# ScalarE issues the query and gate writes, and the bias table follows the state-space parameters

## The chip, the cores and the metric

The kernel runs on one core of a Trainium2 chip. The metric is the device time of one execution in microseconds (us), the median over several runs. A profiled execution of the same program gives the trace.

## The reference

One decoder block on 512 tokens of width 1024, in float32. A normalized input is projected to four parts: `u` (512 columns) for a state-space branch (S5), `q` (1024) and `k`, `v` (256 each) for an attention branch, and `gates` (2048). The two branches are gated, merged by one output projection and added to `x`; a second part (product-key experts, PEER) follows, which the change does not touch.

```python
bias = rel_bias_table.astype(jnp.float32)[t5_bucket(jnp.maximum(dist, 0))]
bias = bias.transpose(2, 0, 1).reshape(N_KV_HEADS, Q_PER_KV, ATTN_BLOCK, 2 * ATTN_BLOCK)
...
scores = jnp.where(valid, scores + bias, NEG_INF)
...
bu_re = jnp.einsum('blgc,gpc->blgp', uf, bbar_re)
bu_im = jnp.einsum('blgc,gpc->blgp', uf, bbar_im)
...
_, _, h_re, h_im = lax.associative_scan(
    _complex_scan_combine, (a_re, a_im, bu_re, bu_im), axis=1)
```

The bias depends on the distance of query and key alone: 16 heads by 384 distances, spread to 128 queries by 256 keys.

## The kernel before

Each float32 product is made of three products of a high and a low part (`mm3`, L94 to L96): `hi*hi`, `lo*hi`, `hi*lo`. A weight block of 512 KB is loaded by SP's queue into `raw` (L117, three buffers), ACT casts it to `hi` (L124), and DVE or POOL subtracts to `lo` (L125); hi and lo have three buffers too. A scheduler orders the instructions of each engine before the run, from the order in which the code yields them; each engine then takes its list strictly in order.

The front part, in the order of the code (`front`):

1. `proj_kv` and `rows`: keys, values, and the normalization rows `rx`, `rb`.
2. `bias_table` (L656): three small loads on ACT's queue, a product `rb_p` on PE, an addition on DVE into the tile `rb_m` of 16 partitions by 384 (L666), and one write of `rb_m` to `bias_d` in device memory (L668), each row 128 times over, 3072 KB. `bias_d` is read back at L833 as a skewed table, 2048 KB.
3. `weave` of `proj` and `s5_params` by two rates: `proj_q` (queries; ACT makes `qt` and its square `sq`, L549 and L550, DVE sums, L551, SP's queue writes `qt` to `q_d`, L553), `proj_u` (L495, L500), and `G0` blocks of `proj_gates`; with them the parameters of S5, a long run of small DVE and POOL operations and matmuls `wtr`, `kps` (L417, L426, `tt` L432).
4. `s5_mix`: four chunks, each with eight matmuls `eps` into two PSUM buffers (L449), DVE operations on the tiles `m` (L453 to L472), and matmuls into `yps` (L476, L478). Beside it run the gate blocks, by the rate `G1`. `eps` and `yps` share four PSUM buffers, the gate blocks' `gps` have two of their own.
5. scores, attention, gated linear unit, branches, output projection. Gate blocks that are left run beside the first scores.

`proj_gates` has 16 blocks of 24 products. For each, DVE multiplies `gps` by `rb` into `gt` (L567), ACT takes the tanh (L568), and the block is written to `g_d` (L569). `gt` and `qt` share two buffers (tag e1): a buffer is free when its write has landed.

Memory: the pool `tp` holds the tiles of the parameters (`wrep0` among them) and of the bias table; it is closed when step 3 ends, and the pool `smp` of `s5_mix`, with the tiles `m`, is opened on the same side and takes the same memory.

Of the kernel before, what the change touches and what calls it, by code (L numbers as in the profile page):

```python
# [10 lines left out]
F32 = mybir.dt.float32  # L11
# [20 lines left out]
def run_some(gen, credit, add):  # L32

    credit += add
    while credit > 0:
        c = next(gen, None)
        if c is None:
            return 0.0
        credit -= c
    return credit  # L40


def weave(main, total, other, cost):

    credit = 0.0
    for c in main:
        yield c
        credit += c * cost / total
        while credit > 0:
            c2 = next(other, None)  # L50
            if c2 is None:
                credit = -1e9
                break
            credit -= c2
            yield c2
    yield from other


class Builder:
    RATE_A, RATE_S, RATE_V, RATE_G = 2.2, 0.96, 1.36, 6.0  # L60
    PARTS = 4
    ALONE, MORE, FAR = 96, 2, 6
    G0, S5C, G1, RATE_Q = 0, 70.0, 8.0, 3.0
    DEEP = 3
    AHEAD = 3
    NT0, NT1, KEY = 2, 2, 3
# [474 lines left out]
    def proj_q(self, xh, xl, ssq, qd, pool):  # L541
        nc = self.nc
        ep = self.ep
        for g in range(2):
            def ev_q(j, ps, g=g):
                qt = ep.tile([128, 512], F32, tag="e1", name=self.nm("qt"))
                sq = ep.tile([128, 512], F32, tag="e2", name=self.nm("sq"), bufs=1)
                r = self.rx[:, j:j + 1]
                nc.scalar.activation(qt, ps, AF.Copy, scale=r)  # L549
                nc.scalar.activation(sq, ps, AF.Square, scale=r)  # L550
                nc.vector.tensor_reduce(ssq[:, j, 8 * g:8 * g + 8], sq.rearrange("p (h d) -> p h d", d=64),  # L551
                                        axis=AX.X, op=ALU.add)
                nc.sync.dma_start(out=qd[j, :, 512 * g:512 * g + 512], in_=qt)  # L553
            yield from self.proj_tok(xh, xl, 512 + 512 * g, ev_q)
        rms = pool.tile([128, NT * 16], F32, name="rms")
        nc.vector.tensor_scalar(rms, ssq.rearrange("p a b -> p (a b)"), 1.0 / 64, EPS, op0=ALU.mult, op1=ALU.add)
        self.rq = self.rsqrt(pool, rms, NT * 16).rearrange("p (a b) -> p a b", b=16)

    def proj_gates(self, xh, xl, bg, gd):
        nc = self.nc  # L560
        for m in range(16):
            wh, wl = self.unit_cols(self.i["w_in"], 2048 + m * 128, 128)
            ps = self.gpsum[0].tile([128, T], F32, tag=self.gpsum[1], name=self.nm("gps"))
            for k in range(KD):
                self.mm3(ps, wh[:, k, :], wl[:, k, :], xh[:, k, :], xl[:, k, :], k == 0, k == KD - 1)
            g = self.ep.tile([128, T], F32, tag="e1", name=self.nm("gt"))
            nc.vector.tensor_mul(g, ps, self.rb)  # L567
            nc.scalar.activation(g, g, AF.Tanh, bias=bg[:, m:m + 1], scale=0.5)  # L568
            nc.sync.dma_start(out=gd[m], in_=g)  # L569
            yield 5.2  # L570

    def kv_prep(self, kv, kH, kL, vH, vL, gk):
# [83 lines left out]
    def bias_table(self, pool, dp):  # L656
        nc, I = self.nc, self.i
        tab = pool.tile([32, 16], F32, name="rb_t")
        oh = pool.tile([32, 384], F32, name="rb_o")
        mk = pool.tile([16, 384], F32, name="rb_m")  # L660
        nc.scalar.dma_start(out=tab, in_=I["rel_bias"])
        nc.scalar.dma_start(out=oh, in_=I["bucket_onehot"])
        nc.scalar.dma_start(out=mk, in_=I["band_mask"])
        ps = self.ptr.tile([16, 384], F32, tag="tr", name="rb_p")
        nc.tensor.matmul(ps, tab, oh, start=True, stop=True)
        nc.vector.tensor_add(mk, mk, ps)  # L666
        bd = dp.tile([16, 128, 384], F32, name="bias_d")
        nc.scalar.dma_start(out=bd, in_=mk[:, None, :].to_broadcast([16, 128, 384]))  # L668
        return bass.AP(tensor=bd.tensor, offset=bd.offset + 127, ap=[[383, 128], [128 * 384, 16], [1, 256]])
# [90 lines left out]
    def front(self, hd, ah, ys):  # L760

        tc, nc, I, L = self.tc, self.nc, self.i, self.pool
        R = "right"
        dp = self.dp
        qd = dp.tile([NT, 128, D], F32, name="q_d")
        gd = dp.tile([16, 128, T], F32, name="g_d")
# [23 lines left out]
        with ExitStack() as ss:  # L790
            sp = L(ss, "s5p")
            up = sp.tile([128, 16, 128], F32, name="up")
            self.rx = kp.tile([128, NT], F32, name="rx")
            rb = self.rb

            def rows():
                with tc.tile_pool(name="np", bufs=1, side=R) as np_:
                    xts = [np_.tile([128, D], F32, name=f"n_x{j}") for j in range(NT)]
                    for j in range(NT):
                        nc.sync.dma_start(out=xts[j], in_=I["x"][j * 128:j * 128 + 128, :])  # L800
                    self.rms_rows(np_, xts, self.rx)
                    ps = self.ptr.tile([128, T], F32, tag="tr", name="rb_ps")
                    for j in range(NT):
                        rr = np_.tile([128, 128], F32, tag="rr", name=self.nm("rr"), bufs=2)
                        nc.vector.tensor_copy(rr, self.rx[:, j:j + 1].to_broadcast([128, 128]))
                        nc.tensor.matmul(ps[:, j * 128:j * 128 + 128], rr, self.ident, start=True, stop=True)
                    nc.scalar.copy(rb, ps)

            gates, credit = self.proj_gates(xh, xl, bg, gd), 0.0

            def proj():
                yield from kvs
                yield from self.proj_q(xh, xl, ssq, qd, kp)
                yield from self.proj_u(xh, xl, up)
                for c, _ in zip(gates, range(self.G0)):
                    yield c

            kvs = self.proj_kv(xh, xl, kv, kp, lambda i: self.x_part(i, small["g1"], xh, xl))
            for _ in range(self.ROWS):
                next(kvs)  # L820
            rows()
            with tc.tile_pool(name="tp", bufs=1, side=R) as tp:
                bias_src = self.bias_table(tp, dp)
                S = {}
                for _ in weave(proj(), 82.0 + 5.2 * self.G0, self.s5_params(sp, tp, S), self.S5C):
                    pass
            with tc.tile_pool(name="smp", bufs=1, side=R) as smp:
                for _ in self.s5_mix(smp, S, up, yg):
                    credit = run_some(gates, credit, self.G1)
# [637 lines left out]
```

## Time and profile before

| | |
|---|---|
| median of 3 runs | 1714.58 us (1713.29 to 1715.45) |
| profiled execution | 1712.47 us |
| its span in the trace | 1710.7 us |
| PE busy | 1622.0 us, 95% |
| DVE busy | 1425.3 us, 83% |
| ACT busy | 843.0 us, 49% |
| mean granted clock of PE | 0.986 |

The share of busy time is a mean over stages. The table of stretches gives it stage by stage, with PEclk, the granted clock of PE as a share of full speed. The list of waits says what ended an engine's idle time. In the timeline, a row is an instruction with its start and duration; a bracket gives the idle time ahead of it and what ended that. For a DMA, the view gives the time from issue to landing. An engine with a q behind its name (SPq, ACTq) is the queue from which DMAs are issued.

### The profile page before, as it was taken

How to read it: one execution, taken by the hardware profiler on the slowest of the kernel's cores; microseconds unless marked ns; L12 is line 12 of the kernel's file. 1: busy time of each engine (PE TensorE's matmuls, PEld its weight loads, DVE VectorE, ACT ScalarE, POOL GpSimd, SP SyncE). 2: the span in 40 equal slices, each digit the busy share in tenths (PEclk: the TensorE clock that was granted, in tenths of full speed). 3: DMA queues.
4: the chain of work that ended last, by engine and by line, in shares of the span. 5: the costliest groups of instructions: out<-in, count | busy, mean ns of one | idle time of the engine just before them, and what ended most of it. 6: DMA issues, size and time to landing. Idle time of an engine off the chain costs nothing.

```text
span 1710.7 us, 25112 instructions
## 1 busy us (share of the span) xinstructions
PE 1622.0 (95%) x8831; PEld 1426.4 (83%) x8831; DVE 1425.3 (83%) x2931; ACT 843.0 (49%) x1290; POOL 575.2 (34%) x472
## 2 busy tenths in 40 slices
PE   7789999998999899999899999999999999999998
PEld 5568878786899888898899998888888888888876
DVE  7799768897797999999999767777887777777876
ACT  5256565664565356766678633333333333333332
POOL 2563022233531322222222324344434343334440
PEclk9899999999999999999999999999999999999999
DMA  7823452656654658767769998889989999999885
GB/s 231 154 86 99 129 172 76 191 151 185 221 164 149 229 191 286 259 237 287 277 222 345 355 352 285 304 322 333 362 311 333 325 321 347 328 344 320 308 276 180
DMA packets 236303, 429.62 MB, mean 251 GB/s; under 512 B 17376, under 2 KB 153104, under 8 KB 233104
## 3 DMA queue, kind: packets, MB, share of 16 engines
q1 hardware_dynamic: 174464, 240.73, 42.4%
q0 software_dynamic: 36864, 134.23, 21.7%
q10 hardware_dynamic: 24848, 53.06, 9.5%
q8 instruction: 69, 1.13, 0.3%
q14 instruction: 58, 0.48, 0.1%
HBM read 373.69 MB, written 54.26 MB: 250 GB/s over the span
## 4 chain that ended last, share of the span: by engine, by line
PE 58%; DVE 21%; DMA 3%; issue 2%; ACT 2%; POOL 0%; SPq 0%; DVEq 0%; ACTq 0%; POOLq 0%
PE po L1160 11%; PE po L1161 10%; PE po L1163 10%; PE pa L94 6%; PE pa L96 6%; PE pa L95 6%; DVE lo L125 5%; DVE sp_row L1209 3%; DVE t_s L966 1%; DVE g_oh L1110 1%; ACT hi L124 1%; DVE g_o L1107 1%; DVE g_ol L1109 1%; DVE t_ix L968 1%; DVE t_ix L972 1%
## 5 line engine op out<-in xcount | busy, mean ns | idle before, releaser
L124 ACT CAST hi<-t_raw 128x1024 fp32r<-128x1024 f32 x256 | 269.6, 1053 | 471.7 <-PE pa L95 195.7
L125 DVE TENSOR_TENSOR lo<-t_raw,hi 128x1024 fp32r<-128x1024 f32 x256 | 312.9, 1222 | 64.2 <-ACT hi L124 63.7
L94 PE MATMUL pa<-x2h,hi 128*128 128x384 f32 x1024 | 348.3, 340 | 14.7 <-ACT u_g L1136 12.5
L96 PE MATMUL pa<-x2h,lo 128*128 128x384 f32 x1024 | 348.8, 342 | 10.7 <-DVE lo L125 10.7
L95 PE MATMUL pa<-x2l,hi 128*128 128x384 f32 x1024 | 345.5, 337 | 0.0
L1192 POOL DMA_INDIRECT sp_row<-peer_u,sp_ei x128 | 192.5, 1504 | 407.4 <-DVE sp_row L1209 369.6
L1192 POOL DMA_INDIRECT sp_row<-peer_v,sp_ei x128 | 198.2, 1549 | 359.8 <-DVE sp_acc L1211 331.7
L1160 PE MATMUL po<-hi,v_wh 128*128 128x512 f32 x768 | 303.5, 395 | 3.2 <-ACT v_wh L89 3.2
L1161 PE MATMUL po<-lo,v_wh 128*128 128x512 f32 x768 | 302.5, 394 | 0.0
L1163 PE MATMUL po<-hi,v_wl 128*128 128x512 f32 x768 | 223.4, 394 | 0.0
L94 PEld LDWEIGHTS pa<-x2h,hi 128*128 128x128 f32 x1024 | 194.2, 190 | 21.3 <-ACT u_g L1136 15.1
L96 PEld LDWEIGHTS pa<-x2h,lo 128*128 128x128 f32 x1024 | 194.1, 190 | 16.9 <-DVE lo L125 15.8
L95 PEld LDWEIGHTS pa<-x2l,hi 128*128 128x128 f32 x1024 | 194.1, 190 | 1.5
L1160 PEld LDWEIGHTS po<-hi,v_wh 128*128 128x128 f32 x768 | 143.8, 187 | 37.5 <-ACT v_wh L89 4.1
L1163 PEld LDWEIGHTS po<-hi,v_wl 128*128 128x128 f32 x768 | 143.8, 187 | 35.4
L1161 PEld LDWEIGHTS po<-lo,v_wh 128*128 128x128 f32 x768 | 143.8, 187 | 32.7
L1211 DVE SCALAR_TENSOR_TENSOR sp_acc<-sp_row,sp_a,sp_acc 128x1024 f32<-128x1024 f32 x128 | 163.7, 1279 | 0.2
L90 DVE TENSOR_TENSOR v_wl<-v_w,v_wh 128x384 fp32r<-128x384 f32 x128 | 71.5, 559 | 110.6 <-ACT v_wh L89 110.6
L1209 DVE SCALAR_TENSOR_TENSOR sp_row<-sp_row,xrow 128x1024 f32<-128x1024 f32 x128 | 155.7, 1216 | 5.4 <-DMA sp_row<-peer_u,sp_ei 5.4
L124 ACT CAST hi<-raw 128x1024 fp32r<-128x1024 f32 x88 | 91.8, 1047 | 85.1 <-PE gps L95 15.5
L89 ACT CAST v_wh<-v_w 128x384 fp32r<-128x384 f32 x128 | 65.4, 511 | 135.9 <-DVE v_w L1149 135.9
L125 POOL TENSOR_TENSOR lo<-raw,hi 128x1024 fp32r<-128x1024 f32 x28 | 68.9, 2460 | 118.1 <-ACT hi L124 109.8
(455 smaller groups left out, 2998.7 us busy)
## 6 DMA issues: line engine op xcount, KB each, us to landing
t_raw<-peer_uT SPq DMA_DIRECT2D x128, 512.0 KB, 4.7
t_raw<-peer_v SPq DMA_DIRECT2D x128, 512.0 KB, 5.7
G_d<-g_st ACTq DMA_DIRECT2D x24, 1024.0 KB, 7.1
v_g<-G_d SPq DMA_DIRECT2D x64, 384.0 KB, 7.7
raw<-w_in SPq DMA_DIRECT2D x32, 512.0 KB, 4.2
A_d<-u_g ACTq DMA_DIRECT2D x68, 192.0 KB, 4.9
v_a<-A_d SPq DMA_DIRECT2D x68, 192.0 KB, 7.2
raw<-w_ab SPq DMA_DIRECT2D x64, 128.0 KB, 3.4
```

The source lines that it names most:

```text
L90: self.nc.vector.tensor_sub(lo, src, r32(hi))
L94: mm(out, lh, rh, start=first, stop=False)
L95: mm(out, lh, rl, start=False, stop=False)
L96: mm(out, ll, rh, start=False, stop=last)
L124: self.nc.scalar.copy(hi, raw)
L125: (self.nc.gpsimd if pool_lo else self.nc.vector).tensor_sub(lo, raw, r32(hi))
L1160: mm(po[j][i], wh[:, c], hi[:, hs[i]], start=first, stop=False)
L1161: mm(po[j][i], wh[:, c], lo[:, hs[i]], start=False, stop=False)
L1163: mm(po[j][i], wl[:, c], hi[:, hs[i]], start=False, stop=last)
L1192: nc.gpsimd.indirect_dma_start(out=got[k], out_offset=None, in_=self.i[n], in_offset=bass.IndirectOffsetOnAxis(ap=ei[:, s:s + 1], axis=0))
L1209: nc.vector.scalar_tensor_tensor(r, r, 1.0, xrow, op0=ALU.mult, op1=ALU.mult, accum_out=av[:, s:s + 1])
L1211: nc.vector.scalar_tensor_tensor(acc, r, av[:, s:s + 1], acc, op0=ALU.mult, op1=ALU.add)
```

## The change

Four edits. `G0` goes from 0 to 3: three gate blocks are yielded with the S5 parameters, and the weave's rate follows. The writes of `qt` and `gt` are issued from ACT's queue in place of SP's. `bias_table` is called behind the weave in place of ahead of it. Its tile `rb_m` becomes a part of a tile with the tag wrep0, so it takes a buffer of the parameters that is used no more at that point.

```diff
--- before.py
+++ after.py
@@ -60,7 +60,7 @@
     RATE_A, RATE_S, RATE_V, RATE_G = 2.2, 0.96, 1.36, 6.0
     PARTS = 4
     ALONE, MORE, FAR = 96, 2, 6
-    G0, S5C, G1, RATE_Q = 0, 70.0, 8.0, 3.0
+    G0, S5C, G1, RATE_Q = 3, 70.0, 8.0, 3.0
     DEEP = 3
     AHEAD = 3
     NT0, NT1, KEY = 2, 2, 3
@@ -550,7 +550,7 @@
                 nc.scalar.activation(sq, ps, AF.Square, scale=r)
                 nc.vector.tensor_reduce(ssq[:, j, 8 * g:8 * g + 8], sq.rearrange("p (h d) -> p h d", d=64),
                                         axis=AX.X, op=ALU.add)
-                nc.sync.dma_start(out=qd[j, :, 512 * g:512 * g + 512], in_=qt)
+                nc.scalar.dma_start(out=qd[j, :, 512 * g:512 * g + 512], in_=qt)
             yield from self.proj_tok(xh, xl, 512 + 512 * g, ev_q)
         rms = pool.tile([128, NT * 16], F32, name="rms")
         nc.vector.tensor_scalar(rms, ssq.rearrange("p a b -> p (a b)"), 1.0 / 64, EPS, op0=ALU.mult, op1=ALU.add)
@@ -566,7 +566,7 @@
             g = self.ep.tile([128, T], F32, tag="e1", name=self.nm("gt"))
             nc.vector.tensor_mul(g, ps, self.rb)
             nc.scalar.activation(g, g, AF.Tanh, bias=bg[:, m:m + 1], scale=0.5)
-            nc.sync.dma_start(out=gd[m], in_=g)
+            nc.scalar.dma_start(out=gd[m], in_=g)
             yield 5.2
 
     def kv_prep(self, kv, kH, kL, vH, vL, gk):
@@ -657,7 +657,8 @@
         nc, I = self.nc, self.i
         tab = pool.tile([32, 16], F32, name="rb_t")
         oh = pool.tile([32, 384], F32, name="rb_o")
-        mk = pool.tile([16, 384], F32, name="rb_m")
+        late = pool.tile([128, 4, 4, 32], F32, tag="wrep0", name="rb_m")
+        mk = late.rearrange("p a b c -> p (a b c)")[0:16, 0:384]
         nc.scalar.dma_start(out=tab, in_=I["rel_bias"])
         nc.scalar.dma_start(out=oh, in_=I["bucket_onehot"])
         nc.scalar.dma_start(out=mk, in_=I["band_mask"])
@@ -820,10 +821,10 @@
                 next(kvs)
             rows()
             with tc.tile_pool(name="tp", bufs=1, side=R) as tp:
-                bias_src = self.bias_table(tp, dp)
                 S = {}
                 for _ in weave(proj(), 82.0 + 5.2 * self.G0, self.s5_params(sp, tp, S), self.S5C):
                     pass
+                bias_src = self.bias_table(tp, dp)
             with tc.tile_pool(name="smp", bufs=1, side=R) as smp:
                 for _ in self.s5_mix(smp, S, up, yg):
                     credit = run_some(gates, credit, self.G1)
```

The order of the instructions is shown at three places. First DVE, around the beginning of `s5_mix`; the names are those of the text above, and a wait for DMAHW is one for a DMA that counts on that lane. Before:

```order
L432 TENSOR_TENSOR tt<-kps_1424,di_1437 32x4x32 [waits PE_49]
L432 TENSOR_TENSOR tt<-kps_1424,di_1437 32x4x32 [waits Activation_49] x3
L567 TENSOR_TENSOR gt_1738<-gps_1713,rb 128x512 [waits DMAHW7_49,DMAHW1_49,PE_49]
L453 TENSOR_TENSOR m_381_1756<-eps_1746,co 128x512 [waits DVE_49,PE_49,Pool_49]
L456 TENSOR_TENSOR m_384_1759<-eps_1746,si 128x512
L125 TENSOR_TENSOR lo_1957<-raw_1954,hi_1956 128x1024 [waits DMAHW5_49,Activation_49]
L454 TENSOR_TENSOR m_382_1757<-eps_1751,si 128x512 [waits PE_49]
L455 TENSOR_TENSOR m_383_1758<-eps_1751,co 128x512
L457 TENSOR_TENSOR m_381_1756<-m_381_1756,m_382_1757 128x512 [waits DVE_49]
```

After:

```order
L567 TENSOR_TENSOR gt_1832<-gps_1807,rb 128x512 [waits DMAHW2_49,PE_49]
L667 TENSOR_TENSOR rb_m<-rb_m,rb_p 16x384 [waits DMAHW5_49,PE_49]
L125 TENSOR_TENSOR lo_2062<-raw_2059,hi_2061 128x1024 [waits DMAHW0_49,DVE_49,Activation_49]
L567 TENSOR_TENSOR gt_1951<-gps_1926,rb 128x512 [waits DMAHW4_49,PE_49]
L125 TENSOR_TENSOR lo_2097<-raw_2094,hi_2096 128x1024 [waits DMAHW3_49,DVE_49,Activation_49]
L453 TENSOR_TENSOR m_396_1861<-eps_1851,co 128x512 [waits DMAHW6_49,DVE_49,Pool_49]
L454 TENSOR_TENSOR m_397_1862<-eps_1856,si 128x512
L455 TENSOR_TENSOR m_398_1863<-eps_1856,co 128x512
L456 TENSOR_TENSOR m_399_1864<-eps_1851,si 128x512
L457 TENSOR_TENSOR m_396_1861<-m_396_1861,m_397_1862 128x512 [waits DVE_49]
L567 TENSOR_TENSOR gt_1986<-gps_1961,rb 128x512 [waits DMAHW7_49,PE_49]
L458 TENSOR_TENSOR m_398_1863<-m_398_1863,m_399_1864 128x512 [waits DVE_49]
```

The first operation of `s5_mix`, L453, waited for DVE, PE and POOL and now waits for a DMA lane in place of PE: DMAHW6, the lane on which the built program counts the write of `bias_d`. It stands behind the gate products 4 and 5 and the addition into `rb_m`, and the product of gate 6 (`gt_1986`) behind it. In PE's list, 96 gate products stand ahead of the first `eps` in place of 24, four of them ahead of the last `kps`; all 384 stand ahead of the first scores in place of 288. The second half of the second chunk's `eps` stands behind 62 more gate products.

Second ACT, around the write of `bias_d`. Before, among the keys and values:

```order
L529 ACTIVATE kv<-tps_130,rx 128x2x256
L124 CAST hi_1032<-raw_1030 128x1024
L531 ACTIVATE sq_694<-tps_130,rx 128x256
L668 DMA bias_d<-rb_m 2048x1x384
L103 ACTIVATE rs_s_698<-k_ss 128x16
L124 CAST hi_1096<-raw_1094 128x1024
```

After, among the gate blocks:

```order
L124 CAST hi_427_2061<-raw_426_2059 128x1024
L568 ACTIVATE gt_393_1832<-gt_393_1832,b_gate_s_97 128x512
L669 DMA bias_d_1845<-rb_m_1838 2048x1x384
L569 DMA g_d_86<-gt_393_1832 128x512
L124 CAST hi_432_2096<-raw_431_2094 128x1024
L568 ACTIVATE gt_409_1951<-gt_409_1951,b_gate_s_97 128x512
L569 DMA g_d_86<-gt_409_1951 128x512
L124 CAST hi_448_2200<-raw_447_2198 128x1024
L568 ACTIVATE gt_414_1986<-gt_414_1986,b_gate_s_97 128x512
L569 DMA g_d_86<-gt_414_1986 128x512
```

The bias write is now issued between the tanh of gate 4 (`gt_393_1832`) and the write of that gate, so the writes of gates 4, 5 and 6 follow it on ACT's queue.

Third SP, where the loads of the gate blocks' weights are issued. Before:

```order
L117 DMA raw_1989<-w_in 128x8x128
L117 DMA raw_2093<-w_in 128x8x128
L569 DMA g_d<-gt_1738 128x512
L117 DMA raw_2197<-w_in 128x8x128
L569 DMA g_d<-gt_1846 128x512
L117 DMA raw_2232<-w_in 128x8x128
L569 DMA g_d<-gt_1881 128x512
L117 DMA raw_2421<-w_in 128x8x128
L569 DMA g_d<-gt_1985 128x512
L117 DMA raw_2456<-w_in 128x8x128
```

After:

```order
L117 DMA raw_1920<-w_in 128x8x128
L117 DMA raw_1955<-w_in 128x8x128
L117 DMA raw_2059<-w_in 128x8x128
L117 DMA raw_2094<-w_in 128x8x128
L117 DMA raw_2198<-w_in 128x8x128
L117 DMA raw_2302<-w_in 128x8x128
```

The writes, which stood among the loads, are gone from SP, and each load follows the last.

## Rows read from the trace of the kernel before

**Rows 1.** The page, part 1: busy us (share of span) x instructions, by engine.

```profile
PE 1622.0 (95%) x8831; PEld 1426.4 (83%) x8831; DVE 1425.3 (83%) x2931; ACT 843.0 (49%) x1290; POOL 575.2 (34%) x472
```

**Rows 2.** Table of stretches: us, then PE, PEld, DVE, ACT, POOL busy; PEclk, DMA share, GB/s.

```profile
79.00:86.00 7.00, 7.00 (x25) 5.17 (x25) 6.82 (x30) 2.46 (x5) 0.00 (x0) 0.79 0.37 112
...
100.00:131.00 31.00, 22.31 (x110) 18.14 (x109) 30.03 (x93) 18.94 (x40) 22.10 (x39) 0.92 0.23 73
...
59.00:79.00 20.00, 9.14 (x28) 6.65 (x27) 8.75 (x24) 6.71 (x12) 17.82 (x40) 0.73 0.91 185
79.00:148.00 69.00, 59.83 (x292) 49.23 (x292) 66.18 (x218) 41.55 (x82) 42.76 (x74) 0.93 0.27 81
148.00:228.00 80.00, 79.55 (x436) 68.11 (x435) 69.17 (x115) 48.86 (x103) 8.12 (x11) 1.00 0.48 143
228.00:256.00 28.00, 27.15 (x134) 22.57 (x133) 15.93 (x34) 14.90 (x32) 6.86 (x4) 1.00 0.48 156
```

**Rows 3.** List of PE's waits, 38 to 135 us: total us, times, longest.

```profile
PE tps L94 <- ACT hi L124: 7.4, 1, 7.4
```

**Rows 4.** The bias table's tile: its two DMA issues (ns, start us) and landings.

```profile
L668 ACTq DMA_DIRECT2D bias_d<-rb_m x1: 672/672/672, 38.6 to 38.6; - x1
L833 ACTq DMA_DIRECT2D bias<-bias_d x1: 388/388/388, 209.3 to 209.3; - x1
...
DMA to landing us min/median/max: 9.4/22.9/36.4
```

**Rows 5.** DMA in the stretch 45 to 52 us: packets, MB, share; issues with landing.

```profile
q10 hardware_dynamic: 442, 0.68, 87.9%
...
raw<-w_in SPq DMA_DIRECT2D x2, 512.0 KB, 18.6
```

**Rows 6.** Timeline of ACT and DVE, 59 to 82 us: start, us, operation, idle before.

```profile
60.71 1.04 ACT L124 CAST hi<-raw 128x1024 fp32r<-128x1024 f32 x1 [6.63 <-DMA raw<-w_in]
...
75.69 0.69 ACT L549 ACTIVATE qt<-tps,rx 128x512 f32<-128x512 f32 x1 [10.90 <-DMA q_d<-qt]
...
61.79 1.27 DVE L125 TENSOR_TENSOR lo<-raw,hi 128x1024 fp32r<-128x1024 f32 x1 [3.24 <-ACT hi L124]
...
78.60 1.23 DVE L125 TENSOR_TENSOR lo<-raw,hi 128x1024 fp32r<-128x1024 f32 x1 [8.41 <-ACT hi L124]
```

**Rows 7.** List of SP's queue waits, 0 to 460 us: total us, times, longest.

```profile
SPq L569 <- ACT gt L568: 79.7, 16, 10.8
```

**Rows 8.** List of PE's waits, 148 to 256 us.

```profile
PE glp L94 <- ACT yg_h L89: 0.9, 1, 0.9
PE qtr L597 <- DVE kL L584: 0.4, 1, 0.4
```

**Rows 9.** Timeline of PE around 140 to 156 us, and the first scores.

```profile
142.46 0.49 PE L426 MATMUL kps<-f_re,wrep 128*128 128x128 f32 x2 [0.48 <-DVE tt L432]
...
144.12 0.39 PE L426 MATMUL kps<-f_im,wrep 128*128 128x128 f32 x2
...
147.57 1.95 PE L449 MATMUL eps<-up,el 128*128 128x128 f32 x16
...
153.71 0.39 PE L94 MATMUL gps<-xh,hi 128*128 128x512 f32 x1
...
154.40 0.39 PE L94 MATMUL gps<-xh,hi 128*128 128x512 f32 x1
...
228.48 0.28 PE L620 MATMUL scp<-kH,a_qs 128*128 128x256 f32 x1
```

**Rows 10.** Timeline of DVE, the addition to the table and the first mixing chunk.

```profile
38.00 0.54 DVE L666 TENSOR_TENSOR rb_m<-rb_m,rb_p 16x384 f32<-16x384 f32 x1
...
149.51 0.69 DVE L567 TENSOR_TENSOR gt<-gps,rb 128x512 f32<-128x512 f32 x1
150.12 0.68 DVE L453 TENSOR_TENSOR m<-eps,co 128x512 f32<-128x512 f32 x1
150.72 0.68 DVE L456 TENSOR_TENSOR m<-eps,si 128x512 f32<-128x512 f32 x1
```

## Prediction

> **What bounds the kernel now.** I read the page's busy shares first: TensorE (PE) is busy 95% of the span [rows 1], so time can be won only where PE stands, and is lost wherever something new makes it stand. Next the table of stretches, for the part of the program that the change touches: the input projection and the state-space branch. Between 59 and 79 us PE works 9.14 of 20 us and VectorE (DVE) 8.75, while the DMA engines are busy 0.91 of the time; from 79 to 148 DVE is busy 66.18 of 69 us and PE 59.83; from 148 to 228 PE is busy 79.55 of 80 [rows 2]. So there are three regimes: a hole in which both engines wait for transfers, a stage that DVE sets, and a dense stage that PE sets. The longest of PE's waits there is 7.4 us, for the high part of a raw weight block [rows 3].
>
> What is late in the hole is read from the transfers. The bias table's write, 3072 KB read out of 16 partitions, is issued at 38.6 us and lands 36.4 us later, near 75 [rows 4]. While nothing but this write's queue moves, it carries 0.68 MB in 7 us, 97 GB/s, and two weight blocks issued meanwhile take 18.6 us to land (median) [rows 5]. Hence ScalarE (ACT) waits 6.63 us for a weight block and then 10.90 us for a query write that must leave its buffer, and DVE waits 3.24 and 8.41 us behind ACT's casts [rows 6].
>
> **The change, part by part.**
>
> *Queries and gate blocks written from ACT's queue.* SP's queue stood 79.7 us behind the sixteen tanh of the gate blocks before it could issue their writes [rows 7]. But PE's waits from 148 to 256 us add up to 1.3 us and none is on a raw weight block [rows 8]: three buffers of raw weights hide what SP loses. I cost this edit at nothing while they hide it. The added issues on ACT sit right behind the activation that makes the data, so ACT waits for nothing new; an issue takes about 0.7 us of ACT's queue at most [rows 4], 24 of them 17 us, on an engine that stands over a third of every stretch [rows 2]. Without that slack the issues would come ahead of the weight casts; that is a rival below.
>
> *The bias write leaves the query stage.* The hole of 59 to 79 goes. It gives back at least the longest wait, 7.4 us [rows 3], at most all that PE stands there, 10.9 us [rows 2]. Since DVE sets the next stage and stood 20 − 8.75 = 11.25 us, I take a value near the upper end, 9.5 us. The pair of last kernel products (kps), which DVE's operations release, begins at 142.46 now [rows 9], so at 133.0 then.
>
> *Three gate blocks among the parameters.* The order shows that only four of the new gate products stand ahead of the last kps; 92 follow behind them, then rb_p, then the first eps. Three products take 0.69 us (153.71 to 154.40), one 0.230 [rows 9]. So: kps from 133.0, eight pairs in some 1.9 us (142.46 to 144.12 and the last one's time), to 134.9; 92 × 0.230 = 21.2 us, to 156.1. PE has then done 96 gate products, where it has 24 done now at 147.57. Per se nothing is won or lost: the same products come earlier.
>
> *The bias write in its new place.* rb_p closes at 156.1; the addition takes 0.54 us [rows 10], the write goes out at about 157. If it needs its 36.4 us [rows 4], it lands at 193.4. Behind it stands something that the diff does not say: the memory of the pool tp, in which rb_m now lies on wrep0, is the memory of the mixing stage's m buffers, so DVE's first operation of s5_mix (L453) must wait until the write has read rb_m out. The order shows it as a wait for a DMA lane which that instruction did not have. DVE is in order: all behind L453 waits too, the product of gate 6 among it, and the write of gate 4 stands on ACT's queue behind the bias write, whose landing gate 6's buffer needs.
>
> PE goes on without DVE only as far as its PSUM buffers reach: eps 1.95 us [rows 9] to about 158.2, then 62 gate products (gates 5 and 6, and 14 of gate 7) × 0.230 = 14.3 us, to 172.5. There the second half of the next eps needs the buffer of the first, free once DVE has done four m operations at 0.60 us each (150.12 to 150.72) [rows 10]: 193.4 + 2.4 = 195.8. **PE stands 23.3 us.** A stage after a hole runs at a lower granted clock: 0.79 over the 7 us behind the present one [rows 2]. That is another 0.21 × 7 = 1.5 us, bounds 0 and 3.
>
> *Against now.* At 172.5 PE has done 96 + 62 = 158 gate products and the eps. Now it reaches that at 147.57 + 1.95 + 134 × 0.230 = 180.3. So without the stand the change would lead by 7.8 us (5.7 to 9.2, for the two ends of the hole).
>
> *Nothing left to fill with.* At the first scores, 228.48 [rows 9], PE still has 96 gate products now, 22.1 us of the 27.15 that it works in 228 to 256 [rows 2]. After the change none is left, so the scores' own 5.1 us of PE stand against DVE's 15.93 less four gate products of 0.69, 13.2: at most 8.1 us of waiting, none if the gated linear unit's products fill in. I take 3, nearer the lower end, because PE is held back for only 1.3 us between 148 and 256 now [rows 8].
>
> **Sum:** −7.8 + 23.3 + 1.5 + 3 = +20.0 us on the profiled execution's 1712.47, so 1732.5; the median of the runs lies 2.1 us above that execution, and the forecast is **1734 us**. With all ends on one side: −9.2 + 23.3 + 0 + 0 = +14, and −5.7 + 23.3 + 3 + 8.1 = +29, so 1729 to 1743 for this case.
>
> [...]
>
> **The rivals.**
>
> *1. The write is short in its new place (ends faster).* What it takes from 38.6 on may be the company: weight loads, query writes. The same bytes read the other way, 2048 KB over 128 partitions, land in 9.4 us [rows 4]; 3072 KB at that rate are 14.1 us. Then the write lands at 171, eps are free at 173.5, PE stands 1 us: −7.8 + 1 + 3 = −3.8, so 1711 us by the median. It decides below 157 + 17.8 us, where the stand is 4.8 us and the sum zero. For it: nothing but a queue is shown as the limit. Against it: the queue moved at 97 GB/s while it was alone [rows 5]. [...] Chance 0.10.
>
> *2. ACT's queue is held by the bias write.* A gate write that follows a long write on the same queue may hold ACT at its issue until the queue has room; then the cast of gate 8 is late by up to the whole landing, and PE, once freed at 195.8, does 10 products and waits for cast (1.0), subtraction (1.2) and clock: 4 to 5 us more, 1739 us. For it: ACT already waited 10.90 us for a write of SP's queue [rows 6]. Against: that was a buffer, not an issue, and the bias write itself held ACT for 0.67 us [rows 4]. Chance 0.13.
>
> *3. The gates fill the stage that DVE sets.* From 100 to 131 PE stands 31 − 22.31 = 8.7 us [rows 2]. Were the gates to run there, all behind would come 8.7 us sooner, +11.3, 1726 us. For it: that is where the new code puts them. Against: the order has them behind the kps. Chance 0.09.
>
> *4. The edits cancel.* The hole stays (it is the loads' own doing, not the write's), so no gain of 7.8, and the stand comes on top: +27.8, 1742 us; against it, the loads' 18.6 us when only the write moves [rows 5]. Chance 0.04.
>
> **How the numbers follow.** The forecast's case has 0.64. Only rival 1 is no slower; with the chance that the wait on rb_m covers less than a whole write, I give 0.10 to faster, 0.05 to the same, 0.85 to slower. 0.2%, 3.4 us, is about what a measurement here can tell from no change. For 8 in 10 the range takes in the forecast's own 1729 to 1743, rivals 2 and 3 and half of the ground down to rival 1: 1717 to 1744.
>
> **What would show it.** Right: PE busy in nearly all of 59 to 79; bias_d issued near 157 and landing some 36 us later; DVE idle nearly 30 us before its first L453, with a DMA named; PE idle some 23 us before an eps of the second chunk; the write of gate 4 as late as the bias write. The hole of 100 to 131 stays. Wrong: L453 that follows its eps at once, a bias write under 18 us, PE dense from 140 to 230, or PE waiting on raw weight blocks.

## The result, and the profile after

The changed kernel takes 1741.52 us (median of 5 runs, 1741.17 to 1742.65) against 1714.58 us before: 26.9 us more, ratio 1.0163, 95% interval 1.0149 to 1.0177. The forecast was 1734 us, slower, with 1717 to 1744 as its range. The span of the profiled execution grew by 29.7 us, from 1710.7 to 1740.4.

The table of stretches of the kernel after, the same columns as [rows 2]:

```profile
59.00:79.00 20.00, 16.17 (x68) 12.02 (x67) 19.73 (x59) 8.35 (x15) 18.73 (x40) 0.95 0.27 80
79.00:148.00 69.00, 59.80 (x287) 49.07 (x286) 62.51 (x190) 40.95 (x80) 42.66 (x76) 0.94 0.28 82
148.00:170.00 22.00, 22.00 (x108) 17.79 (x107) 6.11 (x7) 5.17 (x7) 0.00 (x0) 1.00 0.80 159
170.00:200.00 30.00, 7.81 (x32) 6.52 (x31) 7.57 (x13) 3.30 (x4) 0.14 (x2) 0.60 0.84 127
200.00:228.00 28.00, 28.00 (x163) 24.29 (x163) 28.00 (x56) 16.15 (x40) 0.42 (x4) 1.00 0.35 104
...
310.00:450.00 140.00, 121.66 (x658) 101.01 (x657) 117.85 (x199) 74.54 (x171) 40.87 (x19) 0.94 0.49 149
```

The hole of 59 to 79 is gone: PE works 16.17 of the 20 us, where it worked 9.14 [rows 2]. In its place stands a deeper one: from 170 to 200 PE works 7.81 of 30 us, and the mean granted clock of that stretch is 0.60. The lists of waits of DVE and PE from 38 to 280 us name both sides of it (total us, times, longest):

```profile
DVE m L453 <- DMA bias_d<-rb_m: 21.5, 1, 21.5
...
PE eps L449 <- DVE m L455: 22.2, 1, 22.2
```

The timelines of PE, DVE and ACT, after (start, us, operation, and in brackets the idle time and what ended it):

```profile
156.11 2.05 PE L449 MATMUL eps<-up,el 128*128 128x128 f32 x16
...
173.11 0.39 PE L95 MATMUL gps<-xl,hi 128*128 128x512 f32 x1
195.69 2.04 PE L449 MATMUL eps<-up,el 128*128 128x128 f32 x8 [22.19 <-DVE m L455]
...
170.94 1.23 DVE L125 TENSOR_TENSOR lo<-raw,hi 128x1024 fp32r<-128x1024 f32 x1 [6.32 <-ACT hi L124]
193.66 0.69 DVE L453 TENSOR_TENSOR m<-eps,co 128x512 f32<-128x512 f32 x1 [21.49 <-DMA bias_d<-rb_m]
...
156.79 0.68 ACTq L669 DMA_DIRECT2D bias_d<-rb_m  x1
157.51 12.26 ACTq L569 DMA_DIRECT2D g_d<-gt  x1
169.86 1.05 ACT L124 CAST hi<-raw 128x1024 fp32r<-128x1024 f32 x1 [12.94 <-PE gps L96]
```

The bias write goes out at 156.79. L453, whose wait for this write is the 21.5 us above, starts 36.9 us later, at 193.66, and PE resumes at 195.69. This trace does not give the write's landing; in the run e2 below, where the write stands in the same place, it lands 36.3 us after its issue. Besides, ACT's queue is held for 12.26 us at the issue of gate 4's write, right behind the bias write, and the cast that follows (169.86) starts when that issue is done, though the view names PE.

**Two halves.** To compare kernels whose gate blocks stand in different places, I use two marks of each trace: the first score product and the first product of the experts (`pa`). Ahead of the first mark, a gate product that is done already counts for 0.230 us [rows 9]; behind it, one that is left. Before: first score 228.5 with 288 done, first `pa` 527.8. After: 266.5 with 384 done, 557.5. Ahead of the scores the change loses 266.5 − 228.5 − 96 × 0.230 = 15.9 us; behind them (557.5 − 266.5) − (527.8 − 228.5 − 22.1) = 13.8 us. The sum is the 29.7 us of the spans. The prediction had 17.0 (−7.8 + 23.3 + 1.5) and 3.

### The profile page after: what moved, and what is told of

It is laid out like the page before. It is cut to its first block, busy times and chain, and to the rows that moved or that the text cites. A ratio compares the mean times of both kernels' runs of the same rounds, so it can differ in the third digit from the quotient of the medians.

```text
span 1740.4 us, 25119 instructions
## 1 busy us (share of the span) xinstructions
PE 1630.0 (94%) x8831; PEld 1432.4 (82%) x8831; DVE 1434.2 (82%) x2932; ACT 842.7 (48%) x1290; POOL 576.6 (33%) x471
## 4 chain that ended last, share of the span: by engine, by line
PE 63%; DVE 24%; DMA 6%; ACT 3%; issue 3%; POOL 0%; SPq 0%; ACTq 0%; DVEq 0%; POOLq 0%
PE po L1161 10%; PE po L1162 10%; PE po L1164 10%; PE pa L96 6%; PE pa L94 6%; PE pa L95 6%; DVE lo L125 5%; DVE sp_row L1210 2%; DMA bias_d<-rb_m 2%; PE gps L94 1%; PE gps L96 1%; PE gps L95 1%; DVE t_s L967 1%; DVE g_oh L1111 1%; ACT hi L124 1%
```

## The experiments

All are compared with the kernel before on the same chip, whose median was 1712.8 to 1714.9 us. The two halves are worked out as above from the profile of each run, one execution against one execution of the kernel before; since executions of one kernel lie up to 8 us apart, halves that differ by 1 to 2 us are not told apart.

| run | what it is | us | ratio, 95% interval | products left at the scores | ahead | behind |
|---|---|---|---|---|---|---|
| after | the change | 1741.5 | 1.0149 to 1.0177 | 0 | 15.9 | 13.8 |
| e1 | after, `rb_m` in memory of its own | 1741.7 | 1.0146 to 1.0180 | 24 | 16.4 | 13.8 |
| e2 | after, gate writes on SP | 1741.8 | 1.0151 to 1.0185 | 0 | 14.5 | 14.6 |
| e3 | e1 and e2 | 1729.9 | 1.0081 to 1.0115 | 24 | 5.8 | 9.3 |
| e4 | after, table on 128 partitions | 1719.2 | 1.0028 to 1.0056 | 0 | −7.4 | 13.0 |
| e5 | after, G0 = 0 | 1735.5 | 1.0121 to 1.0155 | 68 | 18.7 | 3.1 |
| e6 | after, table in front | 1724.8 | 1.0053 to 1.0086 | 24 | 1.0 | 10.7 |
| e7 | before, table on 128 partitions | 1709.3 | 0.9972 to 0.9991 | 96 | −4.5 | 0.3 |
| e8 | before, writes on ACT | 1719.4 | 1.0028 to 1.0061 | 96 | 4.6 | −0.1 |
| e9 | e4, G1 = 2 | 1730.4 | 1.0080 to 1.0119 | 102 | 14.4 | 2.7 |
| e10 | e4, G0 = 0, G1 = 6 | 1727.6 | 1.0063 to 1.0100 | 106 | 6.3 | 10.0 |
| e11 | before, G0 = 3 | 1726.0 | 1.0054 to 1.0094 | 24 | 0.1 | 10.7 |
| e12 | e4, G0 = 0 | 1714.1 | 0.9987 to 1.0005 | 68 | −2.9 | 4.6 |

### Which lock holds the stage: e1, e2, e3

Theory A: L453 waits until the write has read `rb_m`. Theory B: ACT, held at its issue, is the cause. e1 gives `rb_m` memory that no tile of the mixing stage lies on:

```diff
-    def bias_table(self, pool, dp):
+    def bias_table(self, pool, dp, own):
...
-        late = pool.tile([128, 4, 4, 32], F32, tag="wrep0", name="rb_m")
-        mk = late.rearrange("p a b c -> p (a b c)")[0:16, 0:384]
+        mk = own.tile([16, 384], F32, name="rb_m")
...
-                bias_src = self.bias_table(tp, dp)
+                bias_src = self.bias_table(tp, dp, sp)
```

> The changed kernel with rb_m in the pool s5p, which no tile of the mixing stage lies on. Theory A (DVE's first m operation waits until the write has read rb_m out, and with gate 4's write behind the bias write on ACT's queue there is a second lock): the 21.5 us wait of L453 goes, but the product of gate 6 waits for gate 4's write instead, so a stand of PE of 14 to 20 us stays, later in the list; 24 gate products are left beside the first scores; 1733 us (1727 to 1738). Theory B (ACT, held 12.26 us at the issue of gate 4's write, is the cause): ACT's queue is as it was, 1741 us (1739 to 1744).

e2 takes the gate writes off ACT's queue:

```diff
-            nc.scalar.dma_start(out=gd[m], in_=g)
+            nc.sync.dma_start(out=gd[m], in_=g)
```

> The changed kernel with the gate writes on SP's queue again, so that nothing follows the bias write on ACT's queue. Theory A: L453 waits for the write as before, PE's stand stays 21 to 23 us, 1741 us (1737 to 1744). Theory B: ACT is no longer held, the stand loses 10 us or more, 1731 us or less.

e3 makes both edits.

> Both edits of the two runs above. Theory A: neither lock is left, no wait for bias_d on DVE, no stand of PE over 3 us between 140 and 230 us; 22 us of stand and 2 us of clock go, and a little of the loss beside the scores (24 gate products are left for them): 1714 us (1710 to 1720). Theory B: no more than the better of the two single edits.

Measured: 1741.7, 1741.8 and 1729.9 us. Neither single edit helps, both together give 11.6 us. The waits from 130 to 300 us (PE's from 38) say why. e1:

```profile
PE gps L94 <- DVE gt L567: 12.5, 1, 12.5
PE yps L478 <- DVE m_hr L471: 4.7, 2, 2.4
...
DVE gt L567 <- DMA g_d<-gt: 23.2, 2, 21.4
```

e2:

```profile
PE eps L449 <- DVE m L455: 21.8, 1, 21.8
...
DVE m L453 <- DMA bias_d<-rb_m: 27.2, 1, 27.2
```

e3:

```profile
PE yps L478 <- DVE m_hi L472: 9.9, 1, 9.9
...
DVE gt L567 <- DMA g_d<-gt: 13.3, 1, 13.3
...
ACT hi L124 <- DMA raw<-w_in: 12.3, 1, 12.3
```

Each lock alone is enough. The time of e1 by itself lies in theory B's range; e2 decides: there nothing follows the bias write on ACT's queue, and PE's stand is the same, 21.8 us. So theory B falls, and the hold of ACT is hidden in the longer wait. In e1 L453 no longer waits for the write, and DVE stands 21.4 us for gate 4's write, whose issue follows the bias write on ACT's queue: the bias write lands at 196.3 us (160.6 and 35.7), and DVE goes on at 197.34. I expected 1733 us from PE's shorter stand; it is 12.5 us and not 22, but the rest came back: the bias write goes out at 160.6 in place of 156.8, and there are small waits, as that on `m_hr`. In e3 there is a third lock: the bias write moves from 158.1 us on, for 37.1 us, and DVE waits 13.3 us for a gate write and ACT 12.3 us for a weight load, both of which go by SP's queue; from 170 to 200 the DMA engines are busy 0.98 of the time and DVE works 15.85 of 30 us. That is the hole of [rows 6] again, in a new place, and I had left it out of the 1714 us expected.

### The write's length: e4

```diff
+        tw = pool.tile([32, 16, 8], F32, name="rb_w")
...
-        mk = late.rearrange("p a b c -> p (a b c)")[0:16, 0:384]
+        mk = late.rearrange("p a b c -> p (a b c)")[:, 0:384]
...
-        nc.scalar.dma_start(out=mk, in_=I["band_mask"])
-        ps = self.ptr.tile([16, 384], F32, tag="tr", name="rb_p")
-        nc.tensor.matmul(ps, tab, oh, start=True, stop=True)
+        nc.scalar.dma_start(out=mk, in_=I["band_mask"][:, None, :].to_broadcast([16, 8, 384]))
+        nc.vector.tensor_copy(tw, tab[:, :, None].to_broadcast([32, 16, 8]))
+        ps = self.ptr.tile([128, 384], F32, tag="tr", name="rb_p")
+        nc.tensor.matmul(ps, tw.rearrange("p a b -> p (a b)"), oh, start=True, stop=True)
...
-        nc.scalar.dma_start(out=bd, in_=mk[:, None, :].to_broadcast([16, 128, 384]))
+        nc.scalar.dma_start(out=bd.rearrange("h (r c) d -> (h r) c d", r=8), in_=mk[:, None, :].to_broadcast([128, 16, 384]))
```

> The changed kernel with the table made on 128 partitions (each head's row on 8 of them), so the same 3072 KB are written from 128 partitions in place of 16. Theory A with the write's length set by its 16 source partitions: it lands in 9 to 15 us, the stand of PE falls to 0 to 3 us, 1718 us (1714 to 1722), above the kernel before by the loss beside the scores less the gain of the query stage. If the length is set by the bytes or by the writes into device memory, it stays 36 us and the time 1741 us (1738 to 1744).

Measured 1719.2 us. The table's tile in e4 (ns and start us; the landings are those of the read, the median and the write), and DVE's wait:

```profile
L671 ACTq DMA_DIRECT2D bias_d<-rb_m x1: 586/586/586, 156.4 to 156.4; - x1
...
DMA to landing us min/median/max: 10.3/12.1/13.8
...
DVE m L453 <- DMA bias_d<-rb_m: 4.7, 1, 4.7
```

The same bytes from 128 partitions land in 13.8 us in place of 36.4, and PE no longer waits for an `eps` at all. Ahead of the scores e4 is 7.4 us in front of the kernel before: the lead of 7.8 us that the prediction worked out for the change without its stand. So the stand comes from the write's 16 partitions; and the 13 us behind the scores are still there, with no stand to blame.

### What is lost behind the scores: e5, e6, e11, e9, e10, e12

The score products `scp` read queries that DVE prepares (`a_qs`), and DVE takes the scores out of their PSUM buffers (`a_sc`). The changed kernel's PE waits for both, from 266.5 to 497 us:

```profile
PE scp L620 <- DVE a_sc L621: 8.7, 11, 3.0
PE scp L620 <- DVE a_qs L603: 4.6, 2, 3.4
```

The kernel before, from 228.5 to 467 us:

```profile
PE scp L620 <- DVE a_sc L621: 3.3, 4, 1.2
```

That is 10.0 us more, 13.3 against 3.3; other waits of PE became shorter. All of PE's time between the two marks, after and then before (columns as in [rows 2]):

```profile
266.50:557.50 291.00, 264.93 (x1624) 231.50 (x1623) 247.66 (x588) 166.86 (x360) 98.19 (x60) 0.96 0.50 153
228.50:527.80 299.30, 280.14 (x1719) 244.47 (x1718) 247.16 (x596) 173.95 (x368) 98.12 (x61) 0.98 0.53 160
```

PE stands 26.1 us after and 19.2 before, 6.9 more. It is busy 264.9 us after and, less the 22.1 us of gate products, 258.1 before, another 6.9 for the same products, at a mean granted clock of 0.96 in place of 0.98 (0.94 from 310 to 450 above). So half of the 13.8 us are waits and half are products that take longer. Theory C: gate products left at the first scores fill these waits. e5 sets G0 back:

```diff
-    G0, S5C, G1, RATE_Q = 3, 70.0, 8.0, 3.0
+    G0, S5C, G1, RATE_Q = 0, 70.0, 8.0, 3.0
```

> The changed kernel with G0 at 0 again: no gate block among the parameters; the table still follows them and the writes are on ACT's queue. 24 gate products stand ahead of the first eps, 68 are left at the first scores. The write goes out at about 141, lands at 177; PE stands some 22 us from about 158. If the loss of 13 us behind the first scores comes from having no gate products left there, it shrinks to about 4: 1732 us (1728 to 1736). If that loss comes from the late table alone, 1741 us (1738 to 1744).

Measured 1735.5 us: the stand is there (PE waits 24.9 us for an `eps`), the loss behind the scores is 3.1 us. e6 puts the table in front again:

```diff
-        late = pool.tile([128, 4, 4, 32], F32, tag="wrep0", name="rb_m")
-        mk = late.rearrange("p a b c -> p (a b c)")[0:16, 0:384]
+        mk = pool.tile([16, 384], F32, name="rb_m")
...
+                bias_src = self.bias_table(tp, dp)
                 S = {}
...
-                bias_src = self.bias_table(tp, dp)
```

> The changed kernel with the bias table ahead of the parameters again, in its old tile; three gate blocks among the parameters and the writes on ACT's queue stay. No stand on bias_d near 160 to 195, the hole at 59 to 79 is back. 24 gate products are left at the first scores. If few gate products left cost 10 to 13 us behind the first scores: 1724 us (1719 to 1729). If that loss comes from the late table: 1713 us (1710 to 1716).

Measured 1724.8 us, loss 10.7: the late table is not its cause. e11 changes G0 alone in the kernel before (0 to 3).

> The kernel before with G0 at 3 and nothing else: 96 gate products ahead of the first eps, 24 left at the first scores, the table in front, the writes on SP's queue. e6 less e8 gives 5.4 us for it; theory C: 1718 us (1715 to 1722), with about 10 us lost behind the first scores and part of that won ahead of them. If it is the writes on ACT's queue that make the loss behind the scores: 1710 us (1706 to 1713).

Measured 1726.0 us, more than expected, with the same loss of 10.7 and nothing won ahead of the scores (0.1). So the three gate blocks alone bring this loss, without the other edits. Then the direct test of theory C, e9: e4 with gate blocks held back (G1 from 8.0 to 2.0).

> The run e4 (changed kernel, table on 128 partitions, 1719.2 us) with G1 at 2 in place of 8: fewer gate blocks are given out beside s5_mix, so 102 gate products are left at the first scores in place of none. Theory C (the 13 us behind the first scores are lost because no gate products are left to fill PE's waits there): most of the 13 us come back, 1707 us (1704 to 1711). Rival (the loss comes from the late table or the order of the attention's own work): 1719 us (1716 to 1722); if the mixing stage now waits for want of filler, above 1722 us.

Measured 1730.4 us, as the last clause of the expectation has it. Behind the scores theory C holds, 2.7 us in place of 13.0; but ahead of them 21.8 us are lost, from −7.4 to 14.4. The table of stretches of e9 shows where:

```profile
148.00:180.00 32.00, 24.22 (x125) 19.71 (x123) 15.86 (x27) 9.77 (x11) 2.55 (x3) 0.93 0.73 240
180.00:200.00 20.00, 12.24 (x80) 11.39 (x80) 20.00 (x43) 8.57 (x32) 0.42 (x4) 0.84 0.01 4
```

From 148 to 180 PE stands 7.8 us, most of it ahead of one `yps`; in e4 it works 22.00 of 22 us from 148 to 170 and 28.84 of 30 from 170 to 200. In both L453 waits even for the short write (6.0 and 4.7 us) and DVE's first chunk follows behind it, but in e9 fewer gate products bridge the time. From 180 to 200 DVE is busy throughout, and PE has only 12.24 us of work: there the mixing stage is bound by DVE. It needs the same products as filler. e10 (G0 = 0, G1 = 6.0, in e4) was meant as the middle way.

> The changed kernel with the table on 128 partitions, G0 at 0 and G1 at 6: no hole in the query stage, no stand on the write, 106 gate products left at the first scores. Theories A and C together: 7 to 8 us under the kernel before, 1705 us (1702 to 1708). If the gain of the query stage does not last without the three gate blocks among the parameters: 1709 us or more, as e7.

Measured 1727.6 us: 6.3 us lost ahead, and 10.0 behind, although 106 products are left. So the number of products left does not settle the loss. What goes with it is the order in which the scheduler lays out PE's work from the gated linear unit to the experts. Kernels in which that order is identical lost alike: before, e7 and e8 −0.1 to 0.3; e6 and e11 10.7; after, e2 and e4 13.0 to 14.6. The order of e1 and e3 is identical too, and they lost 13.8 and 9.3, so the order does not settle all of it. Kernels of one order also have the same number left; only e9 and e10 tell the two apart. e12 is e4 with G0 at 0 and has e5's order.

> The changed kernel with the table on 128 partitions and G0 at 0, G1 at 8: from the first gated linear unit product to the experts PE's order of work is that of e5 (68 gate products left at the first scores, 22 score products ahead of the first gated linear unit product). Theory D (what is lost behind the first scores goes with that order of work, e5's 3 us, whatever stands ahead of it): 7 to 8 us won in the query stage and 3 us lost, 1708 us (1705 to 1711), a way past both kernels. Rival (e5's small loss only shows there because its stand let DVE and the loads catch up): 10 us or more lost behind the scores, 1715 us or more. The mixing stage short of filler, as in e10, would add up to 6 us.

Measured 1714.1 us, no difference from before. Behind the scores 4.6 us, near e5's 3.1, as theory D has it (and theory C, with 68 products left in both); but only 2.9 us were won ahead of them. The stretch of e12:

```profile
148.00:180.00 32.00, 27.95 (x141) 23.84 (x140) 23.30 (x43) 10.94 (x19) 0.35 (x4) 0.89 0.62 205
```

and its PE's wait:

```profile
PE eps L449 <- DVE m L455: 4.1, 1, 4.1
```

Even the short write, at 144.5 us now, leaves a wait of 4.1 us, and the mean granted clock of the stretch is 0.89. With both causes taken out, the write's length and the three gate blocks, the changed kernel is back at the time of the kernel before: these two make up the whole of what it loses against that kernel. Why one order loses 3 us and another 10 at nearly the same count (e9 and e10) stays open.

### The other edits alone: e7, e8

e7 makes e4's edit in the kernel before, whose table is in front.

> The kernel before with the table made on 128 partitions and nothing else changed: the write goes out near 39 and lands 10 to 14 us later, so no query write or weight load is late at 59 to 79. Theory (the write's length makes the hole, and the hole costs 7 to 11 us): 1704 us (1701 to 1706). If the hole is the loads' and query writes' own: 1713 us (1711 to 1715).

Measured 1709.3 us, ratio 0.9981 (0.9972 to 0.9991): the one version faster than the kernel before, by 3.5 us, less than the 9 expected. Its stretches:

```profile
59.00:79.00 20.00, 16.12 (x69) 12.01 (x68) 19.73 (x57) 8.15 (x14) 18.80 (x39) 0.97 0.31 93
79.00:148.00 69.00, 56.53 (x280) 47.23 (x280) 65.41 (x194) 41.22 (x80) 45.08 (x79) 0.93 0.26 79
```

The hole is gone, so the write did make it. But the gain of 9 us at the first kps (84.4 for 93.4) is 5.5 at the last (138.5 for 144.0), in the stage that DVE sets.

e8 makes only the writes' edit in the kernel before (L553 and L569 from `nc.sync` to `nc.scalar`).

> The kernel before with the query and gate writes on ACT's queue and nothing else changed. SP's 80 us of waiting for tanh go. Theory (three buffers of raw weights hide that): 1713 us (1710 to 1716), the hole at 59 to 79 as before. If SP's waiting had held loads that PE needs: 1708 us or less. If issues on ACT hold its casts back: 1717 us or more.

Measured 1719.4 us, 6.5 more. By the marks 4.6 us are lost ahead of the scores and none behind them. PE's longest wait in e8 between 38 and 520 us (total us, times, longest), and the timeline of ACT around the hole, the row of the cast that ends this wait in the kernel before as the first:

```profile
PE tps L94 <- ACT hi L124: 8.7, 1, 8.7
...
77.52 1.04 ACT L124 CAST hi<-raw 128x1024 fp32r<-128x1024 f32 x1
...
62.06 0.36 ACTq L553 DMA_DIRECT2D q_d<-qt  x1
...
63.21 3.17 ACTq L553 DMA_DIRECT2D q_d<-qt  x1
66.43 0.69 ACT L550 ACTIVATE sq<-tps,rx 128x512 f32<-128x512 f32 x1 [3.24 <-DVE rs_t L107]
...
77.88 1.04 ACT L124 CAST hi<-raw 128x1024 fp32r<-128x1024 f32 x1
```

With the bias write on the same queue, the issue of a query write holds ACT for 3.17 us, and the square behind it starts when that issue is done. PE's wait is longer, 8.7 for 7.4 us [rows 3], but the cast that ends it comes only 0.36 us later (77.88 for 77.52), so the hold does not explain the loss. It grows in the parameters' stage, whose order is another too: the first kps come 1.1 us later than before (94.5 for 93.4), the last 2.9 to 3.2 (146.9 and 147.4 for 144.0 and 144.2). Its cause stays open. With G0 at 3 the same edit costs nothing that can be told: e6 and e11 differ in it alone, 1724.8 and 1726.0 us.

## Why the prediction was right, and where it was off

- *What bounds the kernel, and the hole of 59 to 79.* Right. The prediction put the last kps pairs 9.5 us earlier; the last of them begins at 133.97, before at 144.12 [rows 9], 10.2 us. e7 shows that the write alone made the hole. It does not confirm the size: with the hole gone and nothing else changed the last kps come 5.5 us earlier, so part of the 10.2 us has another source, which no run isolates, and that 9.5 was so near is partly luck.
- *The bias write in its new place.* Right, nearly to the us: issue about 157 (156.79), L453 free at 193.4 (193.66), PE stopped at 172.5 (173.5, the end of the product at 173.11), resumed at 195.8 (195.69, behind three operations on `m` and not four), a stand of 23.3 us (22.2). e4 takes the stand away by the write's length alone: 13.8 us, where the write takes 36.4 in the kernel before [rows 4] and 36.3 in e2. That the second lock, gate 4's write, is enough by itself is shown by e1; the prediction named it beside the first.
- *Clock behind the stand.* 1.5 us was about right: from 195.7 to 200 us the granted clock is 0.50; from 197.82 to 199.67 the products come every 0.43 us in place of 0.230, and the eight `eps` take 2.04 us where 1.06 were enough at 169.22, about 2 us in all.
- *Ahead of the scores* the sum was +17.0 and came out at +15.9.
- *Nothing left to fill with.* This is the step that failed: "I take 3", and 13.8 us were lost, beyond the upper end of 8.1. The bound looked only at the stretch of 228 to 256, as if the loss had to fall where the products stood. It falls later too (the granted clock is 0.94 from 310 to 450 us): 6.9 us more of PE's waiting, where waits for DVE's part of the scores grew most (13.3 for 3.3 us), and 6.9 us in products that take longer, at a lower granted clock. That the three gate blocks bring it is shown (e11, e5); that they do it by another order of the whole attention is what the runs fit best, and is not shown. The term makes up the difference between 20.0 and the 29.7 us of the spans, with 1.1 us the other way ahead of the scores. That the time lay within the forecast's range all the same is luck as far as this term goes: the other terms came out near the middle of their bounds.
- *Queries and gate blocks written from ACT's queue, at nothing.* For the gate writes that holds in the changed kernel (e2, 1741.8), under a stand that would hide a small cost; with G0 at 3 and the table in front it holds for both kinds (e6 and e11). As an edit of its own it is wrong: e8 is 6.5 us slower, and why is open. The sentence that ACT "waits for nothing new" is wrong as well, as rival 2 feared: an issue behind the bias write held ACT for 12.26 us.
- *The sum.* 1732.5 and 2.1 give 1734.6, which the prediction puts down as 1734.
- *Rivals.* Rival 1, the short write, is e4's case: the time there is 1719, not 1711, by the loss behind the scores. Rival 2's hold is real, 12.26 us, but stands inside the longer wait: its price was nothing. Rival 3: the hole of 100 to 131 stayed, PE busy 23.36 for 22.31 us. Rival 4 did not happen.

## What to carry to other kernels

Before a tile is laid on memory that is used no more, ask what is opened on that memory next, and how long the tile's last reader takes: here a write of 36 us out of 16 partitions stood ahead of the first instruction of the next stage. Look at the long transfer itself first: spread over 128 partitions it took 13.8 us in e4, and that edit alone, in the old place, is the only one of these that won (e7). Independent products that fill one stage are taken from another; count what is left at each later stage, and cost the new order there up to its end.

## What was not expected of the hardware

- An issue behind a long write on ACT's queue held the engine: 12.26 us in the changed kernel, 11.03 in e1, 3.17 in e8, where most issues on that queue take 0.33 us. Not every issue is held: in e8 the first query write behind the same bias write, at 62.06, took 0.36 us and the second, at 63.21, the 3.17. What decides it is not shown.
- Beside the 3072 KB write out of 16 partitions, transfers of other queues came late as well: in the kernel before a weight load took 18.6 us beside it [rows 5] and 4.1 between 150 and 220 us, without it (medians), and in e3 engines waited 13.3 and 12.3 us for transfers of SP's queue. Out of 128 partitions the same bytes landed in 13.8 us in e4, in place of 36.4 [rows 4]. Why 16 partitions are slower is not shown.
